# Accumulating transfers for the weight sums, eight units by halves per layer, and 1/rms in two steps

## The chip, the core and the metric

The kernel runs on one core of a Trainium2 chip. The metric is device microseconds for one execution, as the median of several runs. The engines are named as in the profile: PE is TensorE (matmuls), PEld its weight loads, DVE is VectorE, ACT is ScalarE, POOL is GpSimd, and SP only issues transfers.

## What is computed

Two layers of a decoder trunk on 512 tokens of width 1024, in float32. A layer is a token mixer and then a gated MLP with a causal convolution of width 3 along the tokens; the change is in the MLP (and in how its 1/rms is made):

```python
h = rms_norm(x, ffn_norm_g[l])
u = causal_dwconv(einsum("bsd,df->bsf", h, ffn_w_in[l]), ffn_conv_w[l]) + ffn_conv_b[l]
gate, up = _split(u, (D_FF, D_FF))
x = x + einsum("bsf,fd->bsd", jax.nn.silu(gate) * up, ffn_w_out[l])
```

`ffn_w_in` is 1024 x 5632 (2816 gate and 2816 up columns), `ffn_w_out` is 2816 x 1024.

## The kernel before

**Layout.** The activations stand transposed: 128 features on the partitions, 512 tokens along the free dimension, so x is 8 blocks (`xT`) and the MLP's inner width is 22 blocks. Each float32 operand is split in a rounded part and its remainder (`split`, lines 157 to 167: ACT writes the rounded part `hi`, then DVE subtracts to get `lo`), and a product is three matmuls, hi by hi, hi by lo and lo by hi (`mm3`, lines 150 to 155). Weights are transferred to a `raw` or `fraw` tile of 128 x 1024 and split into a `whi` and a `wlo` tile; there are two of each (line 206), so the split of a weight tile can begin when the matmuls of the tile two places ahead of it have ended.

**The MLP of one layer** (`ffn`) goes through 11 units of two inner blocks each (256 gate and 256 up columns), in the order of `UNITS` (line 59). A "p" unit (`plain`, line 1114) multiplies directly: 4 blocks of 8 x 3 matmuls of 512 columns, 96 matmuls and 4 weight tiles. An "h" unit (`halves`, line 1134) uses a scheme with 7 products of half size in place of 8 (Strassen-Winograd over 2 x 2 blocks: two halves of the 1024 input rows, gate and up): 7 x 24 = 168 matmuls of 256 columns and 7 weight tiles. Four of the seven hold sums of weight blocks; DVE makes them with four additions of 128 x 1024 (`add`, line 1160) from four blocks that SP transfers. The token side's sums `T` are made once per layer (`build_T`, line 1070).

The h unit's products are called here d, p1, b, c, p4, d', b' in the order of its code (lines 1167 to 1187): d starts the bank that d' finishes, b the one that b' finishes, and p1, c and p4 share a third. Gate and up results are then scaled by 1/rms along the tokens (`rrow`), convolved (one ACT operation and two DVE operations of 128 x 512 each, `conv`), gated with silu and split (`up`, tiles `ahi`, `alo`).

**The down-projection** (`down`) adds chunks of six inner blocks (`CHUNKS`) to four blocks of x at a time, 72 matmuls of 512 columns, between the units; the last chunk comes at the end, in the last layer in token-major form (`down_last`).

**1/rms.** The first p unit multiplies unscaled inputs; after its gate blocks it calls `rms` (lines 491 to 509): four matmuls with ones (L496), a chain of six small DVE and ACT operations (L500, L143 to L147), and four matmuls with the identity (L505) that spread 1/rms over the partitions; DVE copies them to `rrow` (L508).

**What sets the order.** A scheduler orders each engine's instructions by the place in the code; `ahead(key)` (line 94) shifts this place by a number from `AHEAD`. Engines run their own instruction streams in order, and wait for each other by semaphores. PSUM has 8 banks (`acc`), used in turn. POOL in the MLP only writes two zero columns into each `fu` tile (L1091).

## Time and profile before

| | us |
|---|---|
| median of 3 runs | 1284.41 (1283.18 to 1286.51) |
| the profiled execution | 1285.03 |
| its span, first to last instruction | 1283.3 |
| PE busy in the span | 1256.7 |
| DVE busy in the span | 985.9 |
| ACT busy in the span | 680.7 |
| POOL busy in the span | 73.3 |

The profile is of one execution. Its span is 1.7 us shorter than the execution's own time. "Busy" is the union of an engine's instructions, and those of PE overlap one another; so the rate of PE is read from the starts of instructions, or from the length of a stretch in which it never pauses, not from the mean duration of a matmul. A wait is shown as idle time of the engine just before an instruction, with the instruction that released it. "PEclk" is the granted clock of TensorE, 1.00 for 2.4 GHz and 0.50 for 1.2 GHz.

### The profile page before, as it was taken

How to read it: one execution, taken by the hardware profiler on the slowest of the kernel's cores; microseconds unless marked ns; L12 is line 12 of the kernel's file. 1: busy time of each engine (PE TensorE's matmuls, PEld its weight loads, DVE VectorE, ACT ScalarE, POOL GpSimd, SP SyncE). 2: the span in 40 equal slices, each digit the busy share in tenths (PEclk: the TensorE clock that was granted, in tenths of full speed). 3: DMA queues.
4: the chain of work that ended last, by engine and by line, in shares of the span. 5: the costliest groups of instructions: out<-in, count | busy, mean ns of one | idle time of the engine just before them, and what ended most of it. 6: DMA issues, size and time to landing. Idle time of an engine off the chain costs nothing.

```text
span 1283.3 us, 18340 instructions
## 1 busy us (share of the span) xinstructions
PE 1256.7 (98%) x6824; PEld 1037.9 (81%) x6824; DVE 985.9 (77%) x1719; ACT 680.7 (53%) x1216; POOL 73.3 (6%) x305
## 2 busy tenths in 40 slices
PE   8999999999989999999999999999999999999998
PEld 7898765687889899899879877667787898898897
DVE  6857766685988798798858567667779887987983
ACT  5564587454754454454454465774466454454452
POOL 4300011000000000000030000110000000000000
PEclk9999999999999999999999999999999999999999
DMA  6252100052233333321332511002522242342212
GB/s 188 67 161 68 42 13 24 27 176 82 70 103 103 91 103 103 91 87 37 104 91 75 149 50 57 1 26 73 161 82 71 83 127 71 99 128 70 83 62 82
DMA packets 149929, 108.56 MB, mean 85 GB/s; under 512 B 6700, under 2 KB 144114, under 8 KB 149584
## 3 DMA queue, kind: packets, MB, share of 16 engines
q1 hardware_dynamic: 147968, 104.41, 27.4%
q0 software_dynamic: 1024, 1.68, 0.5%
q8 instruction: 53, 0.87, 0.3%
q10 hardware_dynamic: 848, 1.31, 0.3%
q14 instruction: 36, 0.29, 0.1%
HBM read 105.26 MB, written 2.11 MB: 84 GB/s over the span
## 4 chain that ended last, share of the span: by engine, by line
PE 86%; DVE 6%; ACT 5%; issue 1%; DMA 1%; POOL 0%; ACTq 0%; DVEq 0%; POOLq 0%
PE pacc L154 19%; PE pacc L155 18%; PE pacc L153 18%; PE pacc L1155 18%; PE pw L587 2%; PE pw L537 2%; DVE wlo L162 1%; PE pw L548 1%; PE pw L1036 1%; PE pw L1021 1%; ACT whi L161 1%; PE pw L1041 1%; ACT h L545 1%; PE pw L928 1%; PE pw L812 1%
## 5 line engine op out<-in xcount | busy, mean ns | idle before, releaser
L161 ACT ACTIVATE whi<-raw 128x1024 fp32r<-128x1024 f32 (+4 forms) x163 | 154.4, 947 | 212.4 <-PE pacc L154 123.8
L162 DVE TENSOR_TENSOR wlo<-raw,whi 128x1024 fp32r<-128x1024 f32 (+4 forms) x163 | 177.0, 1086 | 65.9 <-ACT whi L161 59.6
L154 PE MATMUL pacc<-h,whi 128*128 128x512 f32 x544 | 216.7, 398 | 0.0
L155 PE MATMUL pacc<-h,wlo 128*128 128x512 f32 x544 | 216.6, 398 | 0.0
L153 PE MATMUL pacc<-h,whi 128*128 128x512 f32 x544 | 216.2, 397 | 0.0
L1155 PE MATMUL pacc<-T,whi 128*128 128x256 f32 x768 | 140.5, 282 | 0.0
L161 ACT ACTIVATE whi<-fraw 128x1024 fp32r<-128x1024 f32 x84 | 89.3, 1063 | 87.2 <-PE pacc L1155 63.9
L162 DVE TENSOR_TENSOR wlo<-fraw,whi 128x1024 fp32r<-128x1024 f32 x84 | 102.7, 1222 | 35.9 <-ACT whi L161 35.7
L154 PE MATMUL pacc<-alo,whi 128*128 128x512 f32 x320 | 126.6, 396 | 0.0
L155 PE MATMUL pacc<-ahi,wlo 128*128 128x512 f32 x320 | 126.5, 395 | 0.0
L153 PE MATMUL pacc<-ahi,whi 128*128 128x512 f32 x320 | 126.5, 395 | 0.0
L154 PEld LDWEIGHTS pacc<-h,whi 128*128 128x128 f32 x544 | 103.3, 190 | 24.8 <-issue 2.3
L153 PEld LDWEIGHTS pacc<-h,whi 128*128 128x128 f32 x544 | 103.0, 189 | 24.4 <-issue 2.0
L155 PEld LDWEIGHTS pacc<-h,wlo 128*128 128x128 f32 x544 | 103.2, 190 | 22.5 <-issue 0.5
L1155 PEld LDWEIGHTS pacc<-T,whi 128*128 128x128 f32 x768 | 118.5, 188 | 2.2
L1155 PE MATMUL pacc<-h,whi 128*128 128x256 f32 x576 | 105.9, 284 | 6.4 <-ACT tmp L1168 6.4
L1155 PE MATMUL pacc<-T,wlo 128*128 128x256 f32 x384 | 109.0, 284 | 0.0
L1155 PEld LDWEIGHTS pacc<-h,whi 128*128 128x128 f32 x576 | 90.1, 192 | 6.8 <-ACT tmp L1168 6.8
L1099 DVE SCALAR_TENSOR_TENSOR tmp<-fu,fcol,tmp 128x512 f32<-128x512 f32 x128 | 93.8, 746 | 0.6
L154 PE MATMUL pacc<-wlo,h 128*128 128x512 f32 (+2 forms) x256 | 91.6, 359 | 0.1
L155 PE MATMUL pacc<-whi,h 128*128 128x512 f32 (+2 forms) x256 | 90.8, 356 | 0.0
L153 PE MATMUL pacc<-whi,h 128*128 128x512 f32 (+2 forms) x256 | 90.8, 359 | 0.0
(331 smaller groups left out, 2354.0 us busy)
## 6 DMA issues: line engine op xcount, KB each, us to landing
fraw<-in_ffn_w_in_dram SPq DMA_DIRECT2D x48, 512.0 KB, 3.6
raw<-in_ffn_w_in_dram SPq DMA_DIRECT2D x40, 512.0 KB, 3.9
raw<-in_ffn_w_out_dram SPq DMA_DIRECT2D x48, 384.0 KB, 3.2
raw<-in_w_in_dram SPq DMA_DIRECT2D x24, 512.0 KB, 3.9
raw<-in_w_in_dram SPq DMA_DIRECT2D x18, 256.0 KB, 4.3
raw<-in_w_out_dram SPq DMA_DIRECT2D x16, 256.0 KB, 2.8
raw<-in_ffn_w_out_dram SPq DMA_DIRECT2D x8, 512.0 KB, 3.6
raw<-in_w_in_dram SPq DMA_DIRECT2D x8, 352.0 KB, 3.1
```

Of the source, the lines that this page charges most:

```text
L153: mm(out, l[0], r[0], start=start, stop=False)
L154: mm(out, l[0], r[1], start=False, stop=False)
L155: mm(out, l[1], r[0], start=False, stop=stop)
L161: self.tok(nc.scalar.activation(hi, src, AF.Copy))
L162: self.tok(nc.vector.tensor_tensor(lo, src, hi.bitcast(F32), op=OP.subtract))
L537: nc.tensor.matmul(s[:, :n], qT(2 * hp + hh, qt), kT(2 * hp + hh, n), start=True, stop=True)
L545: nc.scalar.activation(mb[:, :n], mb[:, :n], AF.Exp, bias=nm, scale=-1.0, accum_out=lsum[:, i:i + 1])
L548: nc.tensor.transpose(s[:, kb * 128:(kb + 1) * 128], mb[:, kb * 128:(kb + 1) * 128], self.ident)
L587: mm = nc.tensor.matmul(pu[hh * 64:(hh + 1) * 64, kb * 128:], V(hh, kb), P(hh, kb), start=kb == 0, stop=kb == NT - 1, skip_group_check=True)
L812: nc.tensor.matmul(pd[:, hh * 64:(hh + 1) * 64], lm[:, hh, :], xdt[:, hh, :], start=True, stop=True)
L1099: stt(v, u[:, i:i + S], w(i), v, op0=OP.mult, op1=OP.add)
L1155: nc.tensor.matmul(out, ws[x], b[i][y], start=start and i == q == 0, stop=stop and i == 3 and q == 2, skip_group_check=True)
```

## The change

- **Units.** `FFN` replaces `UNITS`: per layer three p units and then eight h units, where there were five and six. Over two layers four units change from p to h.
- **Down-projection.** Chunks of four inner blocks instead of six, each in two halves (four blocks of x, 48 matmuls, two weight tiles of 128 x 1024): one half after the third p unit and one after each h unit but the last. The last six inner blocks come at the end: `down_late` in layer 0 (first the inner blocks 16 to 20, then 20 to 22, for four blocks of x), `down_last` in layer 1.
- **Weight sums.** The four DVE additions of an h unit are gone. A block is transferred by SP as before, and the next block is added to it by a transfer that POOL issues with `accum_op=add`: four per unit. The labels of the blocks are dealt anew (`cut`). Tile P holds first 21 + 22, then 11 is added to it, then 12; tile A11 gets 21 added after it has been split. A sum that goes to a tile already in use waits for DVE to have read that tile (its split), and the split of the new sum waits for the transfer. The products are in a new order, called d, p1, c, b, p4, b', d' here. The loads' place is shifted ahead by 300 (`wl`), and there are 8 `fraw` tiles, not 6.
- **1/rms.** `rms` is a generator; the first p unit asks for its first step after the gate blocks and for the second after the up blocks, and only then scales either.
- **fu.** Four fixed tiles; their zero columns are written once per layer.

```diff
-CHUNKS = ((0, 6), (6, 12), (12, 18), (18, 22))
...
-UNITS = "ppphhphhphh"
-
-ACTS, FU, FRAW, FTMP = 10, 4, 6, 8
+
+FFN = ("p", "p", "p", (0, 4, 0, 4), "h", (0, 4, 4, 8), "h", (4, 8, 0, 4), "h", (4, 8, 4, 8), "h", (8, 12, 0, 4), "h", (8, 12, 4, 8),
+       "h", (12, 16, 0, 4), "h", (12, 16, 4, 8), "h")
+LAST = (16, 20, 22)
+
+ACTS, FU, FRAW, FTMP = 8, 4, 8, 8
...
-AHEAD = dict(w=120, pv=200, spv=200, up=-30, blk=-200, st=-60, pc=-200)
+AHEAD = dict(wl=300, w=120, pv=200, spv=200, up=-30, blk=-200, st=-60, pc=-200)
...
         def rms():
-            with self.ahead("st"):
-                return self.rms(ss, sq)
-
-        return (h, rms) if later else (h, *rms())
+            r = self.rms(ss, sq)
+            for _ in range(2):
+                with self.ahead("st"):
+                    got = next(r)
+                yield got
+
+        if later:
+            return h, rms()
+        *_, got = rms()
+        return (h, *got)
...
         self.rsqrt(m, r)
+        yield
         p = self.pS()
         for t in range(NT):
             nc.tensor.matmul(p[:, t * 128:(t + 1) * 128], r[:, t:t + 1].to_broadcast([128, 128]),
                              self.ident, start=True, stop=True)
         rrow = self.sm.tile([128, S], F32, name=self.uid("rrow"), tag="rrow", bufs=1)
         nc.vector.tensor_copy(rrow, p)
-        return rrow, r
+        yield rrow, r
...
+        fus = [self.ph.tile([128, S + 2], F32, name=self.uid("fu"), tag=f"fu{i}", bufs=1) for i in range(FU)]
+        for u in fus:
+            nc.gpsimd.memset(u[:, 0:2], 0.0)
+
         def fu():
-            u = self.ph.tile([128, S + 2], F32, name=self.uid("fu"), tag="fu", bufs=FU)
-            nc.gpsimd.memset(u[:, 0:2], 0.0)
-            return u
+            fus.append(fus.pop(0))
+            return fus[-1]
...
             for f in range(f0, f0 + m, 2):
-                pss = []
-                self.proj_fm(W, l, range(ND), f * 128, 2, h, lambda b, ps: pss.append(ps))
+                g, u = [], []
+                self.proj_fm(W, l, range(ND), f * 128, 2, h, lambda b, ps: g.append(ps))
+                if row:
+                    for b, ps in enumerate(g):
+                        gate(f + b, block(f + b, ps))
+                else:
+                    next(rms)
+                self.proj_fm(W, l, range(ND), FF + f * 128, 2, h, lambda b, ps: u.append(ps))
                 if not row:
-                    row.append(rms()[0])
-                for b, ps in enumerate(pss):
-                    gate(f + b, block(f + b, ps))
-                self.proj_fm(W, l, range(ND), FF + f * 128, 2, h,
-                             lambda b, ps: up(f + b, block(NF + f + b, ps)))
+                    row.append(next(rms)[0])
+                    for b, ps in enumerate(g):
+                        gate(f + b, block(f + b, ps))
+                for b, ps in enumerate(u):
+                    up(f + b, block(NF + f + b, ps))
...
-            A = {}
-            for key, r0, c0 in (("21", 0, FF), ("22", 4, FF), ("11", 0, 0), ("12", 4, 0)):
-                A[key] = raw()
-                nc.sync.dma_start(A[key], bass.AP(tensor=W.tensor, offset=W.offset + (l * D + r0 * 128) * 2 * FF
-                                                  + c0 + f0 * 128, ap=[[2 * FF, 128], [128 * 2 * FF, 4], [1, 256]]))
-            P = raw()
+
+            cut = {"11": (0, FF), "12": (4, FF), "21": (0, 0), "22": (4, 0)}
+
+            def load(t, key, more=True):
+                r0, c0 = cut[key]
+                src = bass.AP(tensor=W.tensor, offset=W.offset + (l * D + r0 * 128) * 2 * FF + c0 + f0 * 128,
+                              ap=[[2 * FF, 128], [128 * 2 * FF, 4], [1, 256]])
+                with self.ahead("wl"):
+                    if more:
+                        nc.gpsimd.dma_start(t, src, accum_op=OP.add)
+                    else:
+                        nc.sync.dma_start(t, src)
+                return t
+
+            P = load(raw(), "21", False)
+            A11 = load(raw(), "11", False)
+            A12 = load(raw(), "12", False)
+            A22 = load(raw(), "22", False)
+            load(P, "22")
...
-            with self.ahead("w"):
-                add(P, A["21"], A["22"])
-            for j, d in prod(self.wsplit(P), Tm(0, 0), "d", 0, True, False):
-                nc.scalar.copy(s[j][0][:, :n], d)
-            with self.ahead("w"):
-                add(A["21"], A["21"], A["11"])
-            for j, p1 in prod(self.wsplit(A["11"]), B(0, 0), "a", 0, True, False):
-                nc.scalar.copy(s[j][0][:, n:], p1)
-            with self.ahead("w"):
-                add(P, P, A["11"])
-            for j, b in prod(self.wsplit(P), Tm(0, 1), "b", 0, True, False):
-                add(s[j][1][:, :n], b, s[j][0][:, n:])
-            for j, c in prod(self.wsplit(A["12"]), B(1, 0), "a", 0, False, True):
-                nc.scalar.copy(us[j][0][:, 2:2 + n], c)
-            with self.ahead("w"):
-                add(P, P, A["12"])
+
+            w = self.wsplit(P)
+            load(P, "11")
+            for j, d in prod(w, Tm(0, 0), "d", 0, True, False):
+                nc.scalar.copy(us[1][j][:, n:], d)
+            w = self.wsplit(A11)
+            load(A11, "21")
+            for j, p1 in prod(w, B(0, 0), "a", 0, True, False):
+                nc.scalar.copy(s[j][:, :n], p1)
+            for j, c in prod(self.wsplit(A12), B(1, 0), "a", 0, False, True):
+                nc.scalar.copy(us[0][j][:, :n], c)
+
+            w = self.wsplit(P)
+            load(P, "12")
+            for j, b in prod(w, Tm(0, 1), "b", 0, True, False):
+                add(s[j][:, n:], b, s[j][:, :n])
             e = {}
-            for j, p4 in prod(self.wsplit(A["22"]), Tm(1, 1), "a", n, True, True):
+            for j, p4 in prod(self.wsplit(A22), Tm(1, 1), "a", n, True, True):
                 e[j] = p4
+
+            for j, b in prod(self.wsplit(A11), Tm(1, 0), "b", 0, False, True):
+                u = us[1][j]
+                add(u[:, :n], b, s[j][:, :n])
+                add(u[:, n:], u[:, n:], u[:, :n])
+                add(u[:, :n], e[j], u[:, :n])
+                tt(u, u, row[0], op=OP.mult)
+                gate(f0 + j, conv(f0 + j, u, neg=True))
+
             for j, d in prod(self.wsplit(P), B(1, 1), "d", 0, False, True):
-                u = us[j][0][:, 2:]
-                add(u[:, n:], d, s[j][1][:, :n])
+                u = us[0][j]
+                add(u[:, n:], d, s[j][:, n:])
                 tt(u, u, row[0], op=OP.mult)
-                gate(f0 + j, conv(f0 + j, us[j][0]))
-            for j, b in prod(self.wsplit(A["21"]), Tm(1, 0), "b", 0, False, True):
-                x = s[j][1][:, n:]
-                add(x, b, s[j][0][:, n:])
-                u = us[j][1][:, 2:]
-                add(u[:, :n], e[j], x)
-                add(u[:, n:], x, s[j][0][:, :n])
-                tt(u, u, row[0], op=OP.mult)
-                up(f0 + j, conv(NF + f0 + j, us[j][1], neg=True))
+                up(f0 + j, conv(NF + f0 + j, u))
...
+        def down_late(f0, f1, f2, blocks):
+
+            ps = [self.acc() for _ in blocks]
+            for c0, c1 in ((f0, f1), (f1, f2)):
+                per = 1024 // ((c1 - c0) * 128)
+                for b in range(0, len(blocks), per):
+                    m = min(per, len(blocks) - b)
+                    hi, lo = self.wsplit(self.wload(Wo, l, range(c0, c1), (blocks[0] + b) * 128, m * 128))
+                    for s in range(b, b + m):
+                        cs = slice((s - b) * 128, (s - b + 1) * 128)
+                        for k in range(c0, c1):
+                            self.mm3(ps[s], (hi[:, k - c0, cs], lo[:, k - c0, cs]), act[k], k == f0, k == f2 - 1)
+                        if c1 == f2:
+                            d = blocks[s]
+                            tt(self.xT[:, d, :], self.xT[:, d, :], ps[s], op=OP.add)
...
-        todo = []
-        for i, kind in enumerate(UNITS):
-            f0 = 2 * i
-            if kind == "h":
+        f0 = 0
+        for i, u in enumerate(FFN):
+            if u == "h":
                 halves(f0)
+            elif u == "p":
+                plain(f0, 2)
             else:
-                plain(f0, 2)
+                down(u[:2], range(*u[2:]))
+                continue
             if i < 2:
                 build_T((2 * i, 2 * i + 1))
-            if todo:
-                down(*todo.pop(0))
-            for c in CHUNKS:
-                if c[1] == f0 + 2 and c[1] < NF:
-                    todo += [(c, range(0, 4)), (c, range(4, 8))]
-        for t in todo:
-            down(*t)
+            f0 += 2
         if l == DEPTH - 1:
-            down_last(*CHUNKS[-1])
+            down_last(LAST[0], LAST[2])
         else:
-            down(CHUNKS[-1], range(ND))
+            down_late(*LAST, range(0, 4))
+            down((LAST[0], LAST[2]), range(4, 8))
 
     def run(self):
         for l in range(DEPTH):
```

On PE, around 1/rms in layer 0 (`ones` are the matmuls with ones, `ident,rstd` those with the identity, `h,whi` and `h,wlo` the projection), before:

```order
L155 MATMUL pacc_2941<-h_2875,wlo_2938 128x512
L496 MATMUL pacc_2966<-ones_108,tmp_2879 128x2 [waits DVE_49]
L496 MATMUL pacc_2966<-ones_108,tmp_2879 128x2 x3
L505 MATMUL pacc_2980<-ident,rstd_2973 128x128 [waits DVE_49]
L153 MATMUL pacc_3009<-h_2847,whi_3005 128x512 [waits Activation_49]
L154 MATMUL pacc_3009<-h_2848,whi_3005 128x512
```

The same engine in the changed kernel, at the end of the first unit's up blocks:

```order
L156 MATMUL pacc_3025<-h_2876,whi_3021 128x512
L157 MATMUL pacc_3025<-h_2875,wlo_3022 128x512
L504 MATMUL pacc_2974<-ones_108,tmp_2879 128x2 x3
L514 MATMUL pacc_3050<-ident,rstd_2981 128x128 [waits DVE_49]
L155 MATMUL pacc_3131<-h_2847,whi_3127 128x512 [waits Activation_49]
L156 MATMUL pacc_3131<-h_2848,whi_3127 128x512
L157 MATMUL pacc_3131<-h_2847,wlo_3128 128x512
```

One of the four matmuls with ones stands after the gate blocks; the other three, and behind them at once the first matmul with the identity, have moved behind the up blocks (48 matmuls later).

On DVE in an h unit and ahead of it (`wlo` are the splits, `fraw<-fraw,fraw` the sums of weights, `xT` the down-projection's addition), before:

```order
L162 TENSOR_TENSOR wlo_3959<-fraw_3876,whi_3958 128x1024
L1160 TENSOR_TENSOR fraw_3876<-fraw_3876,fraw_3874 128x1024
L162 TENSOR_TENSOR wlo_3989<-fraw_3874,whi_3988 128x1024
L1160 TENSOR_TENSOR tmp_3884<-pacc_3879,tmp_3883 128x256
L1160 TENSOR_TENSOR tmp_3886<-pacc_3882,tmp_3885 128x256
L162 TENSOR_TENSOR wlo_4020<-fraw_3870,whi_4019 128x1024
L162 TENSOR_TENSOR wlo_4048<-fraw_3876,whi_4047 128x1024
L1160 TENSOR_TENSOR fraw_4419<-fraw_4411,fraw_4413 128x1024
```

The same in the changed kernel (`fraw_4205` is the unit's P, `fraw_4207` its A11, DMASW the semaphores of POOL's transfers):

```order
L164 TENSOR_TENSOR wlo_4285<-fraw_4209,whi_4284 128x1024 [waits DMAHW3_49,PE_49,Activation_49]
L1122 TENSOR_TENSOR tmp_4128<-tmp_4128,tmp_4082 128x512 [waits DVE_49]
L1230 TENSOR_TENSOR xT<-xT,pacc_4191 128x512
L164 TENSOR_TENSOR wlo_4315<-fraw_4205,whi_4314 128x1024 [waits DMASW4_49,PE_49,Activation_49]
L164 TENSOR_TENSOR alo_4134<-tmp_4128,ahi_4133 128x512 [waits Activation_49]
L164 TENSOR_TENSOR wlo_4346<-fraw_4211,whi_4345 128x1024 [waits DMAHW4_49,PE_49,Activation_49]
L1192 TENSOR_TENSOR tmp_4220<-pacc_4216,tmp_4220 128x256 [waits PE_49]
L1192 TENSOR_TENSOR tmp_4221<-pacc_4219,tmp_4221 128x256 [waits PE_49]
L164 TENSOR_TENSOR wlo_4374<-fraw_4207,whi_4373 128x1024 [waits DMASW5_49,Activation_49]
L164 TENSOR_TENSOR wlo_4420<-fraw_4205,whi_4419 128x1024 [waits DMASW6_49,PE_49,Activation_49]
```

The sums are gone from DVE, and three of the splits wait for a transfer of POOL. POOL's queue, which held the writes of zero columns, now reads, in the same stretch (`fraw_4205` and `fraw_4207` as above, `fraw_3873` the P of the unit ahead, `fraw_4537` that of the next):

```order
L1166 DMA fraw_3873<-in_ffn_w_in_dram 128x4x256 [waits DMASW0_49,DVE_49]
L1166 DMA fraw_4537<-in_ffn_w_in_dram 128x4x256 [waits DMAHW7_49]
L1166 DMA fraw_4205<-in_ffn_w_in_dram 128x4x256 [waits DMASW7_49,DVE_49]
L1166 DMA fraw_4207<-in_ffn_w_in_dram 128x4x256 [waits DMAHW2_49,DMAHW4_49,DMASW5_49,DVE_49]
L1166 DMA fraw_4205<-in_ffn_w_in_dram 128x4x256 [waits DMASW6_49,DMASW4_49,DVE_49]
```

A unit's first sum stands in this queue ahead of the three later sums of the unit before it.

## Rows read from the trace of the kernel before

**Rows 1.** The page: span, PE's busy time, and the chain that ended last.
```profile
span 1283.3 us, 18340 instructions
...
PE 1256.7 (98%) x6824; PEld 1037.9 (81%) x6824; DVE 985.9 (77%) x1719; ACT 680.7 (53%) x1216; POOL 73.3 (6%) x305
...
PE 86%; DVE 6%; ACT 5%; issue 1%; DMA 1%; POOL 0%; ACTq 0%; DVEq 0%; POOLq 0%
```

**Rows 2.** PE's waits, longest first: total us, times, longest us.
```profile
PE pacc L1155 <- ACT tmp L1168: 6.4, 2, 3.2
PE pacc L505 <- DVE rstd L147: 3.7, 2, 1.9
```

**Rows 3.** Stretches of layer 0's MLP: length, busy us (instructions) by engine, PEclk, DMA.
```profile
306.35:350.39 44.04, 44.04 (x195) 36.14 (x194) 43.52 (x70) 30.66 (x44) 0.90 (x9) 1.00 0.26 75
350.39:375.52 25.13, 21.90 (x169) 21.34 (x168) 22.15 (x30) 13.36 (x20) 0.30 (x3) 0.93 0.27 81
362.10:365.50 3.40, 3.24 (x15) 3.24 (x16) 2.70 (x6) 1.23 (x4) 0.10 (x1) 0.50 0.54 167
392.31:412.48 20.17, 20.17 (x170) 19.96 (x169) 16.39 (x21) 9.94 (x14) 0.00 (x0) 1.00 0.31 102
412.48:429.27 16.79, 16.79 (x75) 13.52 (x73) 16.39 (x27) 8.20 (x11) 0.40 (x4) 1.00 0.44 128
429.27:451.67 22.40, 22.40 (x98) 18.14 (x96) 13.94 (x17) 7.63 (x9) 0.30 (x3) 1.00 0.24 72
451.67:471.81 20.14, 20.14 (x169) 19.95 (x168) 18.01 (x23) 11.57 (x17) 0.10 (x1) 1.00 0.33 103
```

**Rows 4.** Timeline around 1/rms, all engines: start, us, instruction, [idle before <-releaser].
```profile
289.98 1.06 ACT L161 ACTIVATE whi<-raw 128x1024 fp32r<-128x1024 f32 x1 [4.38 <-PE pacc L154]
290.02 0.95 PE L496 MATMUL pacc<-ones,tmp 128*128 128x2 f32 x8
...
291.08 1.23 DVE L162 TENSOR_TENSOR wlo<-raw,whi 128x1024 fp32r<-128x1024 f32 x1
...
292.61 0.16 DVE L147 SCALAR_TENSOR_TENSOR rstd<-sm,rstd 128x4 f32<-128x4 f32 x1
...
292.83 0.49 PE L505 MATMUL pacc<-ident,rstd 128*128 128x128 f32 x2 [1.86 <-DVE rstd L147]
```

**Rows 5.** The same columns as rows 3, just after that wait.
```profile
293.83:297.24 3.41, 3.41 (x9) 2.64 (x8) 0.00 (x0) 0.00 (x0) 0.00 (x0) 0.50 0.45 130
```

**Rows 6.** Timeline of DVE, the copy of 1/rms.
```profile
306.63 0.69 DVE L508 COPY rrow<-pacc 128x512 f32<-128x512 f32 x1 [4.08 <-PE pacc L505]
```

**Rows 7.** The page's groups, splits of h units: out<-in xcount | busy, mean ns.
```profile
L161 ACT ACTIVATE whi<-fraw 128x1024 fp32r<-128x1024 f32 x84 | 89.3, 1063 | 87.2 <-PE pacc L1155 63.9
L162 DVE TENSOR_TENSOR wlo<-fraw,whi 128x1024 fp32r<-128x1024 f32 x84 | 102.7, 1222 | 35.9 <-ACT whi L161 35.7
```

**Rows 8.** DVE's groups by shape, one h unit and its down-projection (392.31 to 429.27).
```profile
L1160 DVE TENSOR_TENSOR fraw<-fraw,fraw 128x1024 f32<-128x1024 f32 x4 | 4.9, 1223 | 0.1
L162 DVE TENSOR_TENSOR wlo<-raw,whi 128x768 fp32r<-128x768 f32 x4 | 3.8, 956 | 0.3
L1197 DVE TENSOR_TENSOR xT<-xT,pacc 128x512 f32<-128x512 f32 x5 | 3.3, 682 | 0.0
```

**Rows 9.** DMA issues: out<-in queue op xcount, KB each, median us to landing.
```profile
fraw<-in_ffn_w_in_dram SPq DMA_DIRECT2D x48, 512.0 KB, 3.6
...
raw<-in_w_in_dram SPq DMA_DIRECT2D x18, 256.0 KB, 4.3
raw<-in_w_out_dram SPq DMA_DIRECT2D x16, 256.0 KB, 2.8
...
big<-in_mla_w_uq_dram POOLq DMA_DIRECT2D x2, 288.0 KB, 4.9
big<-in_mla_w_ukv_dram POOLq DMA_DIRECT2D x2, 256.0 KB, 5.5
...
tmp<-in_ffn_conv_w_dram POOLq DMA_DIRECT2D x2, 44.0 KB, 2.2
```

More of the change, by code (lines that the diff above doesn't have):

```diff
@@ L1145, in halves @@
             Tm = lambda j, c: [tuple(p[:, c * n:(c + 1) * n] for p in T[i, j]) for i in range(4)]
-            s = [(self.tmp(), self.tmp()) for _ in range(2)]
-            us = [(fu(), fu()) for _ in range(2)]
+            s = [self.tmp() for _ in range(2)]
+            us = [[fu()[:, 2:] for _ in range(2)] for _ in range(2)]
             def prod(w, b, k, o, start, stop):
```

12 lines of the change are left out of this document (6 added, 6 removed).

## The prediction

> **What bounds the kernel now.** The page first: PE is busy 1256.7 of 1283.3 us, and 86% of the chain that ended last is PE's [rows 1]. So a change pays if it takes matmul time off PE, or a wait ahead of PE; work taken off DVE pays nothing by itself. Second, PE's waits: two groups in the MLP, 6.4 us in two waits for a copy of ACT (L1168) and 3.7 us in two for 1/rms, one of each per layer [rows 2]. Third, stretches of layer 0's MLP cut where one kind of unit ends and the next begins [rows 3]: an undisturbed p unit lasts 22.40 us, an h unit 20.14 to 20.17 us, a down-projection of 72 matmuls 16.79 us (0.233 us each), all with PE busy throughout. The first h unit lasts 25.13 us, for PE stands still in it and the clock falls to 0.50 for 3.4 us after that. The execution took 1285.03 us, 1.73 more than its span and 0.62 above the median of 1284.41; the sum is made against 1285.03.
>
> **Four units from p to h.** Each saves 22.40 - 20.14 = 2.26 us of PE [rows 3], on the path, if the h unit runs without a pause as it does now. Four times: **-9.0 us**. The down-projections keep their number of matmuls.
>
> **The first h unit.** It loses 25.13 - 20.14 = 5.0 us per layer [rows 3]: a wait of 3.2 us [rows 2] and the slower clock after it. The copy that PE waits for came late because DVE was behind: it was busy 43.52 of the 44.04 us before the unit [rows 3], with scaling and convolution that could not start before 1/rms was there. In the changed kernel half a down-projection comes between, 48 x 0.233 = 11.2 us of PE, in which DVE's new work is two splits and four additions to x, 2 x 1.22 + 4 x 0.68 = 5.2 us [rows 7, 8]. That gives DVE 6.0 us; two sums of weights that stood ahead of the wait are gone, 2.4 us more [rows 8]. Against this, 1/rms comes later. It is copied at 306.63 now [rows 6]; then, PE's up blocks end at about 290.0 + 11.0 = 301.0, the chain of [rows 4] takes 2.8 us more, 16 matmuls and the slow clock 5.4 us, the last matmuls 0.6: 309.8 to 310.6, 3.2 to 4.0 us later. The balance is 8.4 - 4.0 = 4.4 us for a wait of 3.2. I take the wait as gone in both layers, **-10.0 us**, with little to spare (bounds -10 and 0).
>
> **1/rms in two steps.** Now the wait is this: matmuls with ones from 290.02 to 290.97, a split of 1.23 us on DVE between the small operations, 1/rms at 292.77, PE idle for 1.86 us [rows 4], then half clock for 3.41 us, which costs half of that, 1.7 us [rows 5]. The order of the changed kernel puts three of the four matmuls with ones right ahead of the first with the identity. ACT and DVE have the splits of the next two weight tiles at the same place as before, one of which waits for the up blocks' last matmul. So the same chain ends the same wait, 48 matmuls later: **0 us**. If the wait went, 2 x (1.86 + 1.7) = 7.1 us would be gained; one more split in the chain (1.22 us) would cost 2 x 1.2 = 2.4.
>
> **Sums by accumulating transfers.** DVE loses 4 x 1.22 = 4.9 us per h unit. An h unit with its half down-projection takes 20.14 + 11.2 = 31.3 us of PE; DVE has 16.39 + 16.39 = 32.8 us in such a stretch of 36.96 us now [rows 3], less 4.9, and two splits of 1.22 for four of 0.96 [rows 7, 8] take off 1.4: 26.5 us, 85% for 89%. DVE stays covered by PE; this brings nothing.
>
> The price is a wait, and whether it shows depends on one time T, from POOL's start to the landing of 512 KB that are added. A product takes 20.14 / 7 = 2.88 us, a split 1.06 + 1.22 = 2.3 us [rows 7] and may start when the product two places ahead has ended. From the start of the unit: P's second split starts at 2 x 2.88 = 5.8 and ends at 8.1; then POOL sends the third sum (12). The third split may start at 5 x 2.88 = 14.4 and must by 6 x 2.88 - 2.3 = 15.0. So **T may be 6.3 us for nothing, 6.9 us without a stall**. The sum with 11 has more: P's first split ends 3.3 us before the unit (at the start of the down-projection's second tile, 5.6 us ahead, plus 2.3), which leaves 9.1 to 9.6 us; 21 into A11 has 9.2 to 9.8. Each unit's first sum goes out during the down-projection ahead of the unit before it, so POOL's queue holds nothing up. Behind a late split stand, on ACT, the down-projection's first split and the convolution, on DVE the unit's additions out of PSUM.
>
> No transfer that adds is in the trace, so T is bounded. From below: 3.6 us, what SP's 512 KB take; from above: twice POOL's 256 KB, 11.0 us [rows 9]. A small POOL transfer lands in 2.2 us, so of SP's 3.6 about 1.4 to 1.6 are the moving of 512 KB; an addition has the old sum to read too, 1.5 more, and POOL's rows stand 1.2 to 2.7 us above SP's 256 KB rows beside other loads [rows 9]. 3.6 + 1.5 = 5.1, plus 0 to 2.7: 5.1 to 7.8. I take 6.0, since nothing else is being transferred in that part of the unit: **0 us**.
>
> POOL's 256 KB took 5.5 us [rows 9]. The Trainium skill (DMA: Bandwidth & Descriptors, "Anatomy of one DMA — SWDGE (gpsimd) path") gives 2.0 us plus the bytes at 436 GB/s, an estimate of 2.6 us for these; the row stands at twice that. By the page 512 KB would take an estimated 3.2 us and no stall could come; by the row twice over they take 11.0 and the kernel would be slower.
>
> **The end of layer 0.** After the last h unit 48 matmuls (11.2 us) wait for nothing, then the next weight tile's split starts only when the second tile's matmuls have ended, and the last unit's `alo` stands behind that split on DVE. Before, 72 matmuls covered it. About one split on ACT, 1.06 us [rows 7]: **+1.0 us** (0 to 3). In layer 1 transposes of x lie there too: 0.
>
> **Sum.** 1285.03 - 9.0 - 10.0 + 1.0 = 1267.0 us. With the bounds above, T apart: 1259.9 to 1281.4.
>
> **Rivals.**
> - *The third sum comes late* (slower than before). Each of 16 h units then stalls by T - 6.9. At T = 8.0 this is 17.6 us and the gain is gone (1284.6); at 9.0 it is 33.6, and the idle time is as long as the 1.86 us after which the clock fell, so up to 16 x 1.7 = 27 us are added: 1301 to 1328. At 11.0 the two other sums are late too (1.4 and 1.2 us): about 1400. For it: POOL's rows of 4.9 and 5.5 us, and an addition that has more to read. Against it: those rows lie beside other transfers.
> - *The third sum is a little late*, T from 6.9 to 8.0: 1267 to 1285.
> - *The first h unit's wait stays*, since the margin is 1.2 us: 1277.
> - *The change does what it says for 1/rms*: 1260. Against it stands the order of PE.
>
> **Chances.** Forecast (1262 to 1272) 0.51; T between 6.9 and 8.0, 0.12; T over 8.0, 0.25; the first wait stays, 0.07; 1/rms without a wait, 0.05. A measurement of this kernel tells about 0.3%, 3.9 us, from no change: faster is below 1280.6, slower above 1288.3. Faster: 0.51 + 0.07 + 0.05 and 0.07 of the slightly late sum: 0.70. Same: 0.05, from T near 8. Slower: 0.25. The range goes from 1259 to 1298, which takes in T up to 8.75 (1.85 x 16 = 30 us, 1297); beyond it is some 0.18. The forecast's own range is 1262 to 1272.
>
> **What would show it.** The landing time of POOL's 512 KB: right at 6, wrong above 6.9. PE's waits: no L1168 row; a row for L514 of 3.7 us or so in two; a row of the h units' products for ACT's `whi` or DVE's `wlo` means a late sum, and its last releaser would be a transfer. h units of 20.1 us and half down-projections of 11.2 us in stretches; two falls of the clock for four. The prediction is wrong if h units last over 21 us, whatever holds them up.

## The result, and the profile after

The changed kernel takes **1263.71 us** (median of four runs, 1263.29 to 1266.12); the kernel before took 1284.2 beside it. The ratio is 0.984 (0.982 to 0.986): faster by 1.6%. The profiled execution took 1264.11 us with a span of 1262.4, 20.9 less than before [rows 1]. Predicted were 1267.0, within 1259 to 1298, and 1262 to 1272 for the forecast's own case.

The page of the changed kernel first: span, busy time, and the chain that ended last.

```profile
span 1262.4 us, 18848 instructions
...
PE 1239.2 (98%) x7112; PEld 1039.1 (82%) x7112; DVE 960.5 (76%) x1728; ACT 694.7 (55%) x1241; POOL 147.9 (12%) x289
...
PE 89%; ACT 5%; DVE 3%; issue 1%; DMA 1%; POOL 0%; ACTq 0%; POOLq 0%; DVEq 0%
```

PE is still what bounds it; it has 17.5 us less to do (1256.7 before), although it carries out 288 more matmuls (7112 for 6824): in four units 168 matmuls of 256 columns stand for 96 of 512. DVE lost only 25 us: 58.6 us of sums are gone, but the four converted units have more splits and additions, and the smaller chunks of the down-projection mean 16 more additions to x (11 us).

PE's waits (total us, times, longest us), where rows 2 had two groups:

```profile
PE pacc L514 <- DVE rstd L149: 4.2, 2, 2.1
...
PE pacc L155 <- DVE xT L1230: 0.9, 1, 0.9
...
PE pacc L155 <- ACT whi L163: 0.7, 1, 0.7
```

The wait for ACT's copy in the first h unit is gone, without a successor: no row names an h unit's product (L1188). The wait for 1/rms is still there, 2.1 us where it was 1.9. The two other rows are new: a wait for the last addition to x at the start of layer 1, and a late weight split at the end of layer 0.

Stretches (from and to, length; busy us and instructions of PE, PEld, DVE, ACT and POOL; PEclk, DMA share, GB/s): the p phase of each layer, from a place shortly ahead of it (385 matmuls, of which 288 are the three p units'); the first h unit; a later h unit and the half down-projection behind it; the end of layer 0 from the end of its last h unit.

```profile
261.00:350.72 89.72, 87.64 (x385) 72.00 (x384) 66.05 (x105) 49.60 (x71) 2.68 (x2) 0.98 0.55 151
883.90:972.04 88.14, 86.06 (x385) 70.85 (x384) 66.05 (x105) 49.62 (x71) 2.68 (x2) 1.00 0.55 154
361.91:381.93 20.02, 20.02 (x169) 19.88 (x168) 14.83 (x22) 9.77 (x14) 3.83 (x3) 1.00 0.93 181
486.73:506.65 19.92, 19.92 (x170) 19.78 (x168) 15.39 (x23) 10.28 (x15) 3.85 (x3) 1.00 0.96 190
506.65:517.85 11.20, 11.20 (x50) 9.03 (x49) 11.20 (x19) 6.22 (x8) 1.28 (x1) 1.00 0.50 135
600.03:660.71 60.68, 58.62 (x258) 46.65 (x257) 41.80 (x60) 30.84 (x44) 13.19 (x29) 1.00 0.37 98
```

The first h unit lasts 20.02 us for 25.13 before [rows 3], a later one 19.92 for 20.14 to 20.17, a half down-projection 11.20. The same stretches of the kernel before, for the p phases and for the end of layer 0 (there with 24 matmuls more after the last h unit, 24 x 0.233 = 5.6 us):

```profile
261.08:350.39 89.31, 87.45 (x385) 71.83 (x384) 71.37 (x111) 50.90 (x72) 0.90 (x9) 0.98 0.40 118
892.71:982.00 89.29, 87.43 (x386) 71.82 (x384) 71.38 (x111) 50.89 (x72) 0.90 (x9) 0.98 0.40 118
604.85:669.35 64.50, 63.71 (x283) 51.22 (x282) 45.99 (x66) 31.39 (x44) 12.96 (x29) 1.00 0.38 107
```

The landing time of the accumulating transfers, on which the prediction hung (queue, KB each, median us):

```profile
fraw<-in_ffn_w_in_dram POOLq DMA_DIRECT2D x64, 512.0 KB, 6.0
```

And one third sum, of the h unit that begins at 486.73: POOL's start, the split of ACT behind it, and that of DVE (start, us, instruction).

```profile
495.08 1.28 POOL L1166 DMA_DIRECT2D fraw<-in_ffn_w_in_dram  x1 [4.43 <-DVE wlo L164]
```
```profile
501.17 1.06 ACT L163 ACTIVATE whi<-fraw 128x1024 fp32r<-128x1024 f32 x1 [1.77 <-PE pacc L1188]
```
```profile
502.26 1.23 DVE L164 TENSOR_TENSOR wlo<-fraw,whi 128x1024 fp32r<-128x1024 f32 x1 [1.61 <-ACT whi L163]
```

POOL starts 8.35 us into the unit, and the transfer lands about 6 us later, at 14.3. It is not alone in that time: POOL starts the next unit's first sum 2.6 us behind it, and the core's transfers run at 194 GB/s:

```profile
497.65 1.28 POOL L1166 DMA_DIRECT2D fraw<-in_ffn_w_in_dram  x1 [1.28 <-DMA fraw<-in_ffn_w_in_dram]
```
```profile
495.08:501.02 5.94, 5.94 (x53) 5.94 (x52) 3.43 (x5) 2.39 (x3) 2.57 (x2) 1.00 0.94 194
```

ACT's split starts at 14.44, released by PE (the tile's buffer), not by the transfer; DVE's ends at 16.76, and the first matmul that reads the low part is due some 0.2 us after the product begins at 17.2. So the sum is just in time for nothing to wait, with about 0.6 to 0.7 us to spare before PE would stand still.

### The profile page after: what moved, and what is told of

Same layout as the page of the kernel before. It is cut to its first block, busy times and chain, and to the rows that moved or that the text cites. A ratio compares the mean times of both kernels' runs of the same rounds, so it can differ in the third digit from the quotient of the medians.

```text
span 1262.4 us, 18848 instructions
## 1 busy us (share of the span) xinstructions
PE 1239.2 (98%) x7112; PEld 1039.1 (82%) x7112; DVE 960.5 (76%) x1728; ACT 694.7 (55%) x1241; POOL 147.9 (12%) x289
## 4 chain that ended last, share of the span: by engine, by line
PE 89%; ACT 5%; DVE 3%; issue 1%; DMA 1%; POOL 0%; ACTq 0%; POOLq 0%; DVEq 0%
PE pacc L1188 25%; PE pacc L156 17%; PE pacc L157 17%; PE pacc L155 17%; PE pw L596 2%; PE pw L546 2%; PE pw L557 1%; PE pw L1045 1%; PE pw L1030 1%; ACT h L554 1%; PE pw L1050 1%; PE pw L821 1%; PE pw L937 1%; DVE sm L925 1%; DMA tmp<-in_ffn_norm_g_dram 1%
## 5 line engine op out<-in xcount | busy, mean ns | idle before, releaser
L164 DVE TENSOR_TENSOR wlo<-fraw,whi 128x1024 fp32r<-128x1024 f32 x112 | 137.0, 1223 | 73.0 <-ACT whi L163 73.0
L1188 PE MATMUL pacc<-T,whi 128*128 128x256 f32 x1024 | 182.8, 281 | 0.0
L155 PE MATMUL pacc<-h,whi 128*128 128x512 f32 x416 | 165.9, 399 | 0.0
L157 PE MATMUL pacc<-h,wlo 128*128 128x512 f32 x416 | 165.6, 398 | 0.0
L156 PE MATMUL pacc<-h,whi 128*128 128x512 f32 x416 | 165.2, 397 | 0.0
L1188 PEld LDWEIGHTS pacc<-T,whi 128*128 128x128 f32 x1024 | 157.4, 189 | 1.4
L1166 POOL DMA_DIRECT2D fraw<-in_ffn_w_in_dram x64 | 82.4, 1288 | 633.1 <-DVE wlo L164 495.6
L1188 PE MATMUL pacc<-T,wlo 128*128 128x256 f32 x512 | 142.1, 282 | 0.0
L1188 PE MATMUL pacc<-h,whi 128*128 128x256 f32 x768 | 138.3, 281 | 0.0
L1188 PEld LDWEIGHTS pacc<-h,whi 128*128 128x128 f32 x768 | 117.0, 188 | 2.2
L1188 PE MATMUL pacc<-h,wlo 128*128 128x256 f32 x384 | 107.2, 279 | 0.0
L1188 PEld LDWEIGHTS pacc<-T,wlo 128*128 128x128 f32 x512 | 95.6, 189 | 0.0
L157 PEld LDWEIGHTS pacc<-h,wlo 128*128 128x128 f32 x416 | 78.6, 189 | 17.5 <-issue 0.5
```

What stands on the lines that cost most here:

```text
L155: mm(out, l[0], r[0], start=start, stop=False)
L156: mm(out, l[0], r[1], start=False, stop=False)
L157: mm(out, l[1], r[0], start=False, stop=stop)
L164: self.tok(nc.vector.tensor_tensor(lo, src, hi.bitcast(F32), op=OP.subtract))
L1166: nc.gpsimd.dma_start(t, src, accum_op=OP.add)
L1188: nc.tensor.matmul(out, ws[x], b[i][y], start=start and i == q == 0, stop=stop and i == 3 and q == 2, skip_group_check=True)
```

## The experiments

Each ratio is against the kernel before, with its 95% interval.

**The sums on DVE again** (the products' order and all else as changed):

```diff
-            P = load(raw(), "21", False)
+            A21 = load(raw(), "21", False)
...
-            load(P, "22")
+            P = raw()
...
+            with self.ahead("w"):
+                add(P, A21, A22)
             w = self.wsplit(P)
-            load(P, "11")
+            with self.ahead("w"):
+                add(P, P, A11)
...
-            load(A11, "21")
+            with self.ahead("w"):
+                add(A11, A11, A21)
...
-            load(P, "12")
+            with self.ahead("w"):
+                add(P, P, A12)
```

> The changed kernel, but the four sums of an h unit are made by DVE again, from four blocks that SP transfers (same products, same order of products). As predicted (the transfers bring nothing, DVE is covered by PE): 1264 to 1266 us. Rival, DVE is full: the changed kernel's DVE is busy 26.46 of 31.20 us in a unit with its half down-projection (trace of the changed kernel, layer 0, 392.90 to 424.10); 4.9 us of sums make 31.4, so a unit lasts 0.2 to 0.6 us longer and more where DVE comes late to a split: 1268 to 1285. On the shorter h units of the changed kernel (19.93 us where 20.15 was measured before): if the new order of the products made them shorter, units without a wait stay at 19.93; if DVE's additions had made them longer, they are at 20.15 again.

1270.78 us, 0.9886 (0.9871 to 0.9901): 7 us slower than the changed kernel by the medians. Two h units of it, each with its half down-projection:

```profile
390.96:411.32 20.36, 20.26 (x169) 19.96 (x168) 19.79 (x26) 10.98 (x16) 0.00 (x0) 1.00 0.34 105
411.32:422.52 11.20, 11.20 (x51) 9.02 (x49) 11.20 (x18) 5.70 (x8) 0.00 (x0) 1.00 0.30 94
548.27:568.66 20.39, 20.17 (x169) 19.91 (x168) 20.06 (x28) 10.99 (x16) 0.00 (x0) 1.00 0.09 27
568.66:579.85 11.19, 11.19 (x50) 9.02 (x49) 11.19 (x17) 6.11 (x8) 0.00 (x0) 1.00 0.27 94
```

DVE is busy 31.0 of 31.56 and 31.25 of 31.58 us: full, as the rival said. The units last 20.06 to 20.40 us (mean 20.25) for a mean of 19.96 in the changed kernel, and 16 x 0.29 = 4.6 us are about the difference of the two profiled spans (4.3). The five runs below whose units are those of the changed kernel and wait for nothing (plain_pool, late_off, rms_one, rms_early, late6) have means of 19.99 to 20.02, so of the 0.29 us some 0.06 can be the spread between executions. So the transfers do earn something.

The first h unit of each layer, with the sums on DVE:

```profile
359.70:379.77 20.07, 20.07 (x169) 19.93 (x168) 19.20 (x26) 10.31 (x15) 0.00 (x0) 1.00 0.33 105
985.14:1005.21 20.07, 20.07 (x169) 19.93 (x168) 19.20 (x26) 10.30 (x15) 0.00 (x0) 1.00 0.35 107
```

PE never pauses in either, so the old wait stays away without the transfers too.

**Plain transfers on POOL** (four of the seven products of an h unit then use wrong weights, those with P and the one with the new A11; the expectation says three):

```diff
-                        nc.gpsimd.dma_start(t, src, accum_op=OP.add)
+                        nc.gpsimd.dma_start(t, src)
```

> The changed kernel with POOL's transfers writing in place of adding, so three of the seven products of an h unit use wrong weights; everything else is as it was. Theory of the prediction, that reading the old sum costs about 1.5 us: landing after 4.5 us where the changed kernel has 6.0. Rival, that POOL's way of issuing sets the time: 5.7 to 6.0 us as with the addition. In both cases the time is 1264 us within 0.3%, since the third sum comes in time already.

1265.82 us, 0.9853 (0.9837 to 0.9869), the same time within the noise, and the landing fell from 6.0 to 4.0 us:

```profile
fraw<-in_ffn_w_in_dram POOLq DMA_DIRECT2D x64, 512.0 KB, 4.0
```

Adding costs about 2 us of the 6; the prediction had estimated 1.5. The prediction's sentence on the Trainium skill (DMA: Bandwidth & Descriptors, "Anatomy of one DMA — SWDGE (gpsimd) path") had an estimate of 3.2 us for 512 KB: the plain transfer took 4.0, the adding one 6.0.

**The third sum later.** A small operation of POOL on the tile, which changes no value, ahead of the third sum; 1, 2 or 4 of the tile's 4 parts:

```diff
             w = self.wsplit(P)
+            with self.ahead("wl"):
+                x = P[:, 0:1, :]
+                nc.gpsimd.tensor_scalar(x, x, 1.0, None, op0=OP.mult)
             load(P, "12")
```

These are the lines of late_a; late_c has `0:2` and late_b `0:4`. The first run was late_b, with all 4 parts.

> The changed kernel with one more operation on POOL ahead of the third sum's transfer in each h unit (it multiplies the tile of 128 x 1024 by 1.0, after DVE has read it), an estimated 1.5 to 3.5 us by POOL's rows of smaller tiles. Theory: the third sum has about 0.7 us to spare (in the changed kernel its split on DVE ends 16.77 us into the unit, and the second matmul with it is due at 17.4), so each h unit becomes longer by the added time less 0.7, 0.8 to 2.8 us, in all 13 to 45 us over 16 units, and more if the clock falls: 1277 to 1330. Rival, that the sum has much more room than that, or that another wait hides it: 1264 to 1268.

1395.34 us, 1.0852 (1.0834 to 1.0871), far beyond what was expected. The edit did more than delay: behind the longer operation the next unit's first sum took its place ahead of the third sum in POOL's queue, so that two transfers of 512 KB ran at once and the third sum landed 10.3 to 12.1 us after its start wherever a next unit had a sum to send. PE's waits:

```profile
PE pacc L1188 <- ACT whi L163: 90.3, 16, 8.0
PE pacc L1188 <- DVE wlo L164: 8.6, 16, 0.8
```

This shows how the kernel loses its gain and more (8.2 us per unit in the mean) when a sum comes some 9 us late, but not where the limit lies. The two shorter operations left the queue's order as it was.

> The changed kernel with a small operation of POOL on 128 x 256 of the tile ahead of the third sum's transfer, which keeps its place in POOL's queue. By 3.10 us for 128 x 1024 (run late_b) and 0.52 us for 128 x 128 an estimated 0.8 to 1.0 us. Theory, 0.7 us to spare: each h unit lasts 0.1 to 0.4 us longer, 1266 to 1270. Rival, the sum has over 1 us to spare: 1264 within noise.

1276.42 us, 0.994 (0.9922 to 0.9957). The operation and POOL's next start took 1.3 us together (start at 9.67 us into the unit for 8.35), and an h unit with the wait:

```profile
425.07:445.71 20.64, 20.30 (x170) 19.96 (x169) 15.43 (x22) 10.28 (x15) 5.13 (x4) 1.00 0.87 168
```
```profile
440.63 1.06 ACT L163 ACTIVATE whi<-fraw 128x1024 fp32r<-128x1024 f32 x1 [2.90 <-DMA fraw<-in_ffn_w_in_dram]
```

Now the split's last releaser is the transfer, and the unit lasts 20.64 for 19.96. 1.3 us later cost 0.7: **0.6 us were to spare**, which agrees with the 0.6 to 0.7 read from the changed kernel. (POOL's operation took 1.17 us, more than the 0.8 to 1.0 that had been estimated, and in the profiled execution the clock fell after both waits for 1/rms, where it fell after one in the changed kernel's; hence 1276 for 1266 to 1270.)

> As late_a, with 128 x 512: an estimated 1.5 to 1.8 us. Theory: 0.8 to 1.1 us per h unit, 16 times: 1276 to 1282, and the step from late_a to this one is the added time of POOL in full, 0.7 to 0.8 us per unit. Rival, more room than that: below 1272. Rival, that every stall costs more than itself since the clock falls: above 1290.

1311.43 us, 1.0216 (1.0188 to 1.0245), above the 1276 to 1282 of the theory, as its last rival had it. The start was 2.0 us late, and in this place the next unit's first sum starts 0.8 us after the third, so that the third's own landing time rose to a median of 6.8 us. PE's waits are now up to 2.5 us long, and behind some of them the clock falls to half. The waits for ACT's split, and one unit with the stretch after its wait:

```profile
PE pacc L1188 <- ACT whi L163: 14.1, 13, 2.5
```
```profile
465.47:489.32 23.85, 22.09 (x170) 21.54 (x169) 16.92 (x26) 10.17 (x15) 5.78 (x4) 0.93 0.85 176
485.10:488.50 3.40, 3.39 (x16) 3.39 (x17) 3.37 (x7) 0.00 (x0) 0.00 (x0) 0.50 1.13 302
```

Both of the prediction's rivals about the third sum are thereby seen: late by a little, and late with the clock on top of it.

**The half down-projections one place later**, none ahead of the first h unit:

```diff
-FFN = ("p", "p", "p", (0, 4, 0, 4), "h", (0, 4, 4, 8), "h", ...
+FFN = ("p", "p", "p", "h", (0, 4, 0, 4), "h", (0, 4, 4, 8), ...
```

> The changed kernel with the half down-projections one place later: none between the third p unit and the first h unit, one after each h unit, the last of each layer too. Theory of the prediction, that the half down-projection ahead of the first h unit is what covers DVE there: PE waits in the first h unit again; 1/rms is copied 4.5 us later than in the kernel before (311.1 for 306.6), two sums of weights are gone from DVE (2.4 us), so the wait is 3.2 + 4.5 - 2.4 = 5.3 us and 1.7 us of slow clock, twice; 1 to 2 us come back at the end of layer 0: 1275 to 1277. Rival, that the removed sums of weights alone had ended the wait: 1262 to 1264.

1275.9 us, 0.993 (0.9908 to 0.9952), as the theory had it. The first h unit, and PE's waits in it:

```profile
348.67:374.68 26.01, 22.19 (x170) 21.50 (x168) 21.35 (x32) 13.53 (x20) 5.10 (x4) 0.93 0.77 162
```
```profile
PE pacc L1188 <- ACT whi L163: 3.7, 2, 1.9
...
PE pacc L1188 <- ACT tmp L1201: 2.7, 2, 1.4
```

It lasts 26.01 for 20.02 us, with the clock at half for part of it, even a little more than before the change (25.13). PE's waits in it sum to 3.8 us, less than the 5.3 that were expected, and they stand at three places and not at one. The half down-projection ahead of it is what took the wait away: the transfers alone do not (this run), and they are not needed for it (dve_sums).

**Only the units**, in the kernel before:

```diff
-UNITS = "ppphhphhphh"
+UNITS = "ppphhhhhhhh"
```

> The kernel before with three p and eight h units per layer and nothing else changed: whole down-projections after the units as its own list has them, sums of weights by DVE. Theory of the prediction (each unit saves 2.26 us, DVE is covered): 1284.5 - 9.0 = 1275.5. Rival, DVE is behind where two h units stand side by side: an h unit's own work on DVE is 26.3 us (16.39 + 16.39 less 6.5 of the down-projection) for 20.15 us of PE, so up to 6 us are lost at each of the places where that happens: 1280 to 1300.

1317.52 us, 1.0257 (1.0242 to 1.0273): the four conversions that should save 9 us cost 33 when made alone. PE's wait of rows 2 is there six times; and the stretch in which a second h unit stands beside the first:

```profile
PE pacc L1155 <- ACT tmp L1168: 38.5, 6, 8.0
```
```profile
449.27:462.40 13.13, 8.54 (x73) 8.34 (x71) 13.07 (x20) 6.83 (x8) 0.30 (x3) 0.99 0.21 66
462.20:469.00 6.80, 3.17 (x15) 3.17 (x16) 6.08 (x10) 3.27 (x8) 0.10 (x1) 0.50 0.36 121
```

DVE is busy 13.07 of 13.13 us while PE waits, and then the clock is at half for 6.8 us. The kernel before has one down-projection of 72 matmuls behind a unit at most, and two for every three units; so with eight h units in a row an h unit follows another directly at four places over the two layers.

**The end of layer 0 as before:**

```diff
-            down_late(*LAST, range(0, 4))
+            down((LAST[0], LAST[2]), range(0, 4))
```

> The changed kernel without its new order at the end of layer 0: the last six inner blocks go into each of the first four blocks of x at once, 18 matmuls at a time, as in the kernel before. Theory of the prediction: PE then has 12 matmuls (2.8 us) after the last h unit before it needs that unit's output, where the new order gives 48 (11.2 us). In the changed kernel that output (alo) is there 13.0 to 14.3 us after the unit, so PE waits some 10 us once, perhaps 1.7 us of slow clock more: 1272 to 1276. Rival, DVE and ACT finish the unit sooner when PE stands still and the order matters little: 1264 to 1267.

1272.21 us, 0.990 (0.9882 to 0.9919), as the theory had it in sum. The end of layer 0 lasts 5.9 us longer than in the changed kernel (60.68), and this wait stands in it:

```profile
601.80:668.33 66.53, 61.56 (x258) 47.77 (x257) 42.68 (x61) 31.52 (x45) 13.21 (x29) 0.95 0.34 96
```
```profile
PE pacc L155 <- ACT ahi L163: 3.5, 1, 3.5
```

The wait is a third of the 10 us that were expected: the first block of the unit's output is there 9.2 us after the unit, where the changed kernel has it after 12.6, for fewer weight splits stand ahead of it on ACT and DVE. The slower clock (0.95 in the mean) makes up the rest of the 5.9. The medians differ by 8.5, and what lies between that and 5.9 is outside this stretch.

**1/rms in one step again**, after the gate blocks:

```diff
                 else:
                     next(rms)
-                self.proj_fm(W, l, range(ND), FF + f * 128, 2, h, lambda b, ps: u.append(ps))
-                if not row:
                     row.append(next(rms)[0])
                     for b, ps in enumerate(g):
                         gate(f + b, block(f + b, ps))
+                    g = None
+                self.proj_fm(W, l, range(ND), FF + f * 128, 2, h, lambda b, ps: u.append(ps))
                 for b, ps in enumerate(u):
```

> The changed kernel with both steps of 1/rms asked for after the gate blocks, as in the kernel before. Theory of the prediction (the same chain ends the same wait, only 48 matmuls earlier): two waits of 1.9 to 2.1 us at the matmul with the identity, no wait in the first h unit, the same time as the changed kernel, 1262 to 1266. Rival, the two steps had cost or gained something by themselves (4 us of scaling and convolution that DVE starts later, or a shorter chain): more than 2 us away from 1263.7, with the waits at the first h unit or at the identity different.

1264.35 us, 0.9842 (0.9826 to 0.9859): no difference to the changed kernel. Two waits, as before:

```profile
PE pacc L514 <- DVE rstd L149: 3.7, 2, 1.9
```

**The first step of 1/rms earlier**, so that all matmuls with ones stand behind the gate blocks:

```diff
-AHEAD = dict(..., st=-60, pc=-200)
+AHEAD = dict(..., st=-60, st1=0, pc=-200)
...
-            for _ in range(2):
-                with self.ahead("st"):
+            for k in ("st1", "st"):
+                with self.ahead(k):
```

> The changed kernel with the first step of 1/rms placed 60 places earlier: all four matmuls with ones stand right behind the gate blocks, and the small operations of DVE and ACT ahead of the splits of the next two weight tiles. Theory of the prediction, that the wait is the chain behind the three late matmuls with ones: both waits of 2.08 us go, and the fall of the clock after the one in layer 0 (1.7 us): 1258 to 1260. Rival, that 1/rms is late for another reason (the splits, the second step's place): a wait of 1 us or more stays at the matmul with the identity: 1262 to 1264.

**1258.4 us**, 0.9793 (0.9779 to 0.9808), 5.3 less than the changed kernel. Its chain now runs beside the up blocks (the same columns as rows 4):

```profile
290.78 0.95 PE L504 MATMUL pacc<-ones,tmp 128*128 128x2 f32 x8
...
293.18 0.16 DVE L148 SCALAR_TENSOR_TENSOR sm<-sm,rstd 128x4 f32<-128x4 f32 x1
```
```profile
302.69 0.38 PE L514 MATMUL pacc<-ident,rstd 128*128 128x128 f32 x2
```

The matmul with the identity has no wait ahead of it, and L514 is in no row of PE's waits. The clock falls in neither layer.

**On top of that, the end of layer 0 for six blocks** in place of four:

```diff
-            down_late(*LAST, range(0, 4))
-            down((LAST[0], LAST[2]), range(4, 8))
+            down_late(*LAST, range(0, 6))
+            down((LAST[0], LAST[2]), range(6, 8))
```

> The kernel rms_early with the new order at the end of layer 0 for six blocks of x in place of four, so that 72 matmuls (16.8 us) and not 48 (11.2 us) follow the last h unit before its output is needed. Theory: the changed kernel's end of layer 0 lasts 1.8 us longer than before since 11.2 us are too few for that output; with 16.8 that goes: 1258.4 less 1.0 to 1.8, 1256.6 to 1257.4. Rival, the loss lies at the start of the next layer and grows since x is finished closer together: 1258.4 to 1260.

**1257.43 us**, 0.9789 (0.9773 to 0.9805). The stretch, and that of the run rms_early ahead of it:

```profile
596.48:655.78 59.30, 58.27 (x259) 46.73 (x257) 41.29 (x60) 30.80 (x44) 13.03 (x29) 1.00 0.35 101
```
```profile
597.09:657.49 60.40, 58.62 (x258) 46.56 (x257) 41.28 (x60) 30.86 (x44) 13.08 (x29) 1.00 0.35 99
```

1.1 us shorter in the trace; the medians differ by 1.0, which the timing alone would not tell apart. This is the fastest version of the study.

**Nine h units and two p units**, on top of rms_early, with 1/rms spread after the first up block and one half down-projection cut in two pieces (the list of units, its end left out):

```diff
+FFN = ('p', 'p', (0, 4, 0, 2), 'h', (0, 4, 2, 4), 'h', (0, 4, 4, 8), 'h', ...
```

> The kernel rms_early with 1/rms spread over the partitions already after the first up block (its second step's matmuls with the identity right behind it), and nine h units and two p units per layer; one of the half down-projections is cut in two, so that a piece stands ahead of each of the first two h units. Theory: DVE, which stood idle for 4 to 5 us at a time while it waited for 1/rms, starts to scale some 14 us sooner, which makes up for the 8.5 us of room that the third p unit gave it (22.4 us of PE, 13.9 of DVE); two more units save 22.4 - 19.95 = 2.45 us each: 1258.4 - 4.9 = 1253.5. Rival, DVE is late at the first h unit again: a wait of 2 to 6 us and slow clock, twice: 1258 to 1270.

1266.11 us, 0.9855 (0.9838 to 0.9871), 7.7 slower than rms_early: the rival, though without its slow clock. DVE starts to scale sooner, and is full from then on; stretches up to the first h unit, and its first part:

```profile
300.00:316.00 16.00, 16.00 (x72) 13.13 (x71) 15.89 (x26) 13.45 (x19) 0.00 (x0) 1.00 0.31 99
316.00:328.00 12.00, 12.00 (x54) 9.80 (x53) 11.67 (x19) 8.24 (x12) 0.00 (x0) 1.00 0.27 89
328.00:345.00 17.00, 14.20 (x94) 11.90 (x94) 13.69 (x23) 10.38 (x18) 3.83 (x3) 1.00 0.49 93
```

PE then waits 2.8 of 17 us in many small pieces, for the token side's sums, the splits and the second unit's output. From the start of the first piece of the down-projection (325.26) to the end of the first h unit (355.38) 30.1 us pass, where the same matmuls take 25.6 us without a wait (20.0 and half of 11.2). These 4.5 us, twice, are more than the 4.9 that the two units save; they explain most of the difference of the two profiled spans (5.2), and why the median is 2 us worse still is open.

## Why the prediction was right, point by point

The forecast's time was 3.3 us above the median, 2.9 above the profiled execution, and its mechanism is the one that ran, but for the sums, where one step failed and one number was right in part by luck. Its terms against the trace (predicted, measured):

| step | predicted | measured |
|---|---|---|
| four units from p to h | -9.0 | 4 x (19.96 - 22.40) = -9.8 |
| first h unit, both layers | -10.0 | about 2 x (20.02 - 25.13) = -10.2 |
| the other ten h units | 0 | 20.11 to 19.96 in the mean, -1.5 |
| 1/rms, by the p phases | 0 | +0.4 and -1.1: -0.7 |
| the third sum | 0 | no wait: 0 |
| end of layer 0 | +1.0 | 60.68 - (64.50 - 5.6) = +1.8 |
| sum | -18.0 | -20.4 of -20.9 |

The mean length of the changed kernel's 16 h units, 19.96 us, is that of lengths from 19.91 to 20.05; the ten h units before that were not the first of their layer had eight lengths of 20.14 to 20.16 and two of 19.97, 20.11 in the mean.

- **p to h**: right; shown as a saving of PE's time by the stretches. That it can be collected only with the rest of the change is shown by the run with the units alone.
- **First h unit**: right, cause included. Taking away the cover (d_moved) brought the wait back, 12 us for the forecast's 10. Its margin of 1.2 us was mis-sized, without harm. 1/rms was copied 4.5 us later (311.10 for 306.63), not 3.2 to 4.0:

```profile
311.10 0.69 DVE L517 COPY rrow<-pacc 128x512 f32<-128x512 f32 x1 [6.98 <-PE pacc L514]
```

  By the prediction's own sum that leaves 0.7 us, and without the 2.4 us of sums a wait of 1.7. But with the sums on DVE there was none (dve_sums; in its layer 1 the clock had fallen and 1/rms came as long ahead of the first h unit as here), so the margin is at least that much larger; how large was not measured.
- **1/rms in two steps**: right that nothing is gained, since the order of PE put three matmuls with ones at the end; one step gives the same time, and moving them takes the wait away. The bound of 7.1 us for that stands above the 5.3 found, as the clock had fallen in one layer only. The text "two falls of the clock for four" was wrong for this execution: in the MLP there was one.
- **The sums, T**: 6.0 predicted, 6.0 measured, which is partly luck. The prediction chose 6.0 "since nothing else is being transferred in that part of the unit", and that was not so: SP's loads and the next unit's first sum were under way. That first sum does not go out during a down-projection, as the prediction had it, but 10.3 to 11.2 us into the unit before its own, close behind the third sum; in late_b it got ahead of it. And the parts were off both ways: adding costs 2.0 us for 1.5, a plain transfer of POOL takes 4.0 us for the 4.5 left in the sum. POOL started at 8.35 and not at 8.1, so of the 0.9 us left between 6.0 and 6.9 some 0.6 remained, as the runs with a later sum show. The rival "third sum late" was a real danger, not a formal one: in late_c a start 2.0 us later, and a landing 0.8 us slower, left the kernel 27 us slower than before, the clock's part included.
- **The sums, DVE**: this step failed. "DVE stays covered by PE; this brings nothing" was argued from the busy share of the new kernel, and was not asked of the new order without the transfers. There DVE would have 26.5 + 4.9 = 31.4 us in 31.2 (19.96 + 11.2), and the run with the sums on DVE is 4 to 7 us slower. The sum of the prediction did not suffer, as the transfers were in it.
- **The other ten h units** became 0.15 us shorter, a term that was not in the sum; by the 19.99 to 20.02 of the five other runs it is 0.09 to 0.15 us. With DVE's sums back in place the units are at 20.25, and how this divides between the order of the products and DVE is open.
- **End of layer 0**: the mechanism named (the split of the next weight tile waits for the second tile's matmuls, and the last unit's low part stands behind it on DVE) is in the trace as the 0.7 us wait for `whi`, and late6 takes this wait away; the term was 0.8 us too small, since the next layer's start came to it: PE waits there 0.9 us for the last addition to x (L1230) and 0.4 for 1/rms, where the kernel before had one wait of 0.8. It is within the 0 to 3 that was given.
- **The bounds**: the lower one, 1259.9, kept the end of layer 0 at +1.0; with that term at its own bound of 0 it is 1258.9. Nothing hangs on it here.
- **Not tested by themselves**: the loads' place 300 ahead, the eight `fraw` tiles and the fixed `fu` tiles.

## What to carry to other kernels

A conversion that saves time on the bounding engine is worth only as much as the helper engine can follow, place by place: the same four units cost 33 us alone and save 9.8 by their lengths (8.6 with the weight sums still on DVE) once an independent piece of work stands between any two of them. Work given to a transfer has to be priced by its latency against the place where it is needed; here the slack was 0.6 us, in 16 places: 1.3 us later cost 12.7 of the 20.5 us gained, and the next step later cost all of them and more. When a step is split so that it can run beside other work, look at the order in which the engine really gets its instructions: one number for the place of four small matmuls was worth 5 us more.

## What the runs showed of the hardware

- In the h units of the changed kernel an accumulating transfer of 512 KB to SBUF landed 5.7 to 6.5 us after POOL's start, when no other accumulating one had been started in the 5 us ahead of it. One that was started 1.9 to 2.8 us behind another took 8.0 to 9.6 us, and the one ahead kept its time. With 0.8 us between the two (late_b) the one ahead took 7.1 to 8.6 and the one behind 10.3 to 12.1. A plain one of POOL's (plain_pool) took 3.8 to 5.1 us by the same measure, 4.9 to 5.7 close behind another.
- POOL was busy 1.28 us with each start of an accumulating transfer, and 0.75 with a plain one.
- The same wait of 2.1 us ahead of the same matmul was followed by a fall of the clock in one layer and not in the other. In the changed kernel, the stretches after the two waits:

```profile
305.00:308.40 3.40, 3.40 (x10) 2.65 (x9) 0.00 (x0) 0.00 (x0) 0.00 (x0) 0.51 0.48 141
928.00:931.40 3.40, 3.40 (x18) 2.81 (x17) 0.00 (x0) 0.00 (x0) 0.00 (x0) 1.00 0.49 144
```

With d_moved and dve_sums it was layer 1 that fell and not layer 0, with late_a both, and with plain_pool both for 6.8 us each. Half clock costs half of its stretch, so a wait of this kind cost an estimated 0, 1.7 or 3.4 us beyond itself from one execution to the next, and a sum should carry it as a range.
